# Seven products for eight on a second group of 512 columns of the MLP's second projection, with six PSUM banks holding sums

## The chip, the cores and the metric

The kernel runs on one core of one Trainium2 chip. The metric is the device time of one execution in microseconds. A core has a matrix engine (TensorE, PE in the profile; its weight loads are PEld), a vector engine (VectorE, DVE), a scalar engine (ScalarE, ACT), GpSimd (POOL) and SyncE (SP), which here only starts the loads of the weights. Each engine works off its own list of instructions in a fixed order and waits for the others by semaphores. TensorE writes its sums to PSUM, which has eight banks of 128 x 512 float32 values; VectorE and ScalarE read them from there.

## The reference

Two layers on x of 256 rows and 2048 columns, all in float32. What matters here is the MLP at the end of each layer:

```python
D_MODEL, SEQ, DEPTH, D_FF = 2048, 256, 2, 4 * 2048
for l in range(DEPTH):
    ...                                   # attention and gMLP, output projection, residual
    h2 = rms_norm(x, norm2_g[l])
    x = x + jnp.square(jax.nn.relu(h2 @ w_up[l])) @ w_down[l]
return rms_norm(x, final_g)
```

`w_up` is 2048 x 8192, `w_down` is 8192 x 2048. The result is x of 256 x 2048.

## The kernel before

**Data and precision.** x is kept turned, as `x[128, 16, 256]`. Each float32 operand is split into a high part in the type fp32r and a low part, the remainder. A product of two matrices is made of three products: high by high, high by low, low by high. The weights come in tiles `raw` of 128 x 1024 (512 KB) by SyncE's queue. ScalarE makes the high part (`hi`, L152, or L170 for half a tile), VectorE the low part (`lo`, L162 or L175). There are six buffers for `raw`, seven for `hi`, six for `lo`.

**Steps.** The program is a list `steps`, in the order of TensorE's work. An *ordinary step* (`transposed`) uses one weight tile: 4 blocks of rows by 256 columns, the weights stationary, 24 products of 128 x 128 by 128 x 256 (L380, L382, L384). A bank of PSUM takes the sums of 256 columns: four ordinary steps for `w_up`, two for `w_down`. Then the bank is read: after `w_up` by VectorE at L715, followed by L716, a copy by ScalarE (L611) and a subtraction (L612), together called the *evacuation* here; after `w_down` by the update of x (L471). Ordinary sums rotate through four banks, `acc`.

**Eighths.** The hidden width of 8192 is taken in eight parts of 1024, called eighths, e = 0 to 7. The loop over e puts the 16 up steps of eighth e (numbered 0 to 15) ahead of the down steps of eighth e-1, so that the hidden values are ready in time; e = 8 has the last down steps alone.

**Seven products for eight.** For the first 512 columns of `w_down` the kernel does not multiply directly. Over a pair of row blocks it takes the Winograd form of Strassen's rule: two matrices of 2 x 2 blocks are multiplied with seven block products in place of eight. `fast` makes this of *quick steps*, two in each eighth (a *pair*), with one ordinary step between them. A quick step loads two tiles (`Top`, `Bottom`) and makes two more out of them in place (`Sums`, four subtractions by VectorE, L202, L203, L205, L206). It has 42 products, with the hidden values stationary (L408, L410, L411). So it has one half-tile high and low part and three full ones. The sums of the hidden values that the rule needs are made once an eighth (`sums`, L729 to L732, and four calls of `to_half` into `shared`). The seven block sums lie in the four banks `aux`, half a bank each, and are added up in place through all eight eighths. After the last, `combine` (L744 to L751) makes the four blocks of the result with one copy and seven additions, and `turn_back` turns them by eight transposes (L760), in two sets of four, for the update of x.

**The order of the work.** It is written out by the loop at the end. At each step ScalarE's high parts are put down up to six tiles ahead and VectorE's low parts up to five tiles ahead of `done`, the tiles used so far; a quick step counts as four. Then come the step's products, and what follows the step (`after`: an evacuation, an update). Longer follow-ups lie in `queue` with a number of tiles to let pass (`later`, about one of them a step) or in `due` (`soon`, run ahead of the low parts). VectorE works strictly in this order: an evacuation that waits for TensorE holds up the low parts behind it.

```python
            rest = up or down
            at = {1: (10, 11), 8: (0, 1)}.get(e, (6, 7))
            for i, one in enumerate(rest):
                if quick and i in at:
                    steps.append(quick.pop(0))
                steps.append(one)
```

So a pair stands ahead of up steps 6 and 7 (10 and 11 for e = 1).

## Time and profile before

| | |
|---|---|
| time, median of 3 runs (lowest to highest) | 2054.35 us (2054.31 to 2054.35) |
| the profiled execution, its own time | 2054.54 us |
| its span | 2052.8 us |
| mean granted clock of TensorE in it | 0.998 |
| an eighth, from one pair to the next | 86.0 us (479.87 to 565.86) |
| bytes read from HBM | 390.65 MB, 191 GB/s over the span |

The profile shows one execution. Busy times are the time in which an engine had an instruction at work; the chain that ended last follows the work back from the last instruction to what released it. In rows of the timeline stand the start, the duration, the engine, the line of the code, the instruction, what it writes and reads, and in brackets the idle time ahead of it and what ended it. Products of TensorE overlap: each lasts 0.28 us there, and one starts every 0.11 us.

### The profile page before, as it was taken

Reading aid. Unit: us, or ns where it says so; the run is one execution under the profiler, and the core shown is the slowest. Engines: PE = TensorE matmul, PEld = TensorE weight load, DVE = VectorE, ACT = ScalarE, POOL = GpSimd, SP = SyncE. Lnnn points to the kernel's source line nnn. Section 1 sums busy time; section 2 is a strip of 40 time slices with the busy share of each in tenths; the row PEclk is TensorE's granted clock in tenths of the full one; section 3 lists DMA queues with packets and bytes.
Section 4 is the critical chain, followed back from the end, with each engine's and each line's share of the span. In section 5 each row is a group of like instructions: output and inputs, shape, how many; then the busy total and the mean of one; then the engine's idle time right before and its main releaser. Section 6 shows DMA issues by size and latency. Waiting matters only on the chain.

```text
span 2052.8 us, 40389 instructions
## 1 busy us (share of the span) xinstructions
PE 2040.6 (99%) x17066; PEld 2004.3 (98%) x17066; DVE 1464.6 (71%) x1800; ACT 1009.3 (49%) x1265; POOL 68.0 (3%) x90
## 2 busy tenths in 40 slices
PE   9999999999999999999999999999999999999997
PEld 8998999999999999999989989999999999999997
DVE  7666766777687776877866667668777777777776
ACT  7555454454354443544545654544444544445444
POOL 0002300000000000000000032000000000000000
PEclk9999999999999999999999999999999999999999
DMA  8555555565565655556564555555655756556553
GB/s 317 187 165 174 186 188 193 170 224 193 174 214 178 224 187 184 206 180 211 182 237 159 172 184 177 194 196 172 218 192 168 235 190 202 185 175 224 194 179 113
DMA packets 112118, 395.38 MB, mean 193 GB/s; under 512 B 12352, under 2 KB 16448, under 8 KB 111936
## 3 DMA queue, kind: packets, MB, share of 16 engines
q1 hardware_dynamic: 110800, 389.86, 56.8%
q8 instruction: 133, 2.18, 0.4%
q10 hardware_dynamic: 1136, 2.94, 0.4%
q14 instruction: 49, 0.40, 0.1%
HBM read 390.65 MB, written 2.10 MB: 191 GB/s over the span
## 4 chain that ended last, share of the span: by engine, by line
PE 99%; DVE 0%; DMA 0%; ACT 0%; ACTq 0%; issue 0%; DVEq 0%
PE acc L384 27%; PE acc L382 27%; PE acc L380 27%; PE acc L431 3%; PE acc L433 3%; PE acc L432 3%; PE aux L408 3%; PE aux L411 3%; PE aux L410 3%; PE aux L657 0%; PE aux L601 0%; PE aux L559 0%; PE aux L588 0%; DVE x L876 0%; DMA x<-in_xT 0%; PE aux L562 0%
## 5 line engine op out<-in xcount | busy, mean ns | idle before, releaser
L152 ACT ACTIVATE hi<-raw 128x1024 fp32r<-128x1024 f32 (+1 forms) x773 | 784.1, 1047 | 397.3 <-PE acc L384 211.8
L162 DVE TENSOR_TENSOR lo<-raw,hi 128x1024 fp32r<-128x1024 f32 (+1 forms) x773 | 907.8, 1213 | 42.5 <-ACT hi L152 22.9
L380 PE MATMUL acc<-hs,hi 128*128 128x256 f32 x2816 | 781.5, 278 | 0.0
L384 PE MATMUL acc<-hs,hi 128*128 128x256 f32 x2816 | 779.1, 277 | 0.0
L382 PE MATMUL acc<-hs,lo 128*128 128x256 f32 x2816 | 779.1, 277 | 0.0
L380 PE MATMUL acc<-half,hi 128*128 128x256 f32 x2048 | 566.6, 277 | 0.0
L384 PE MATMUL acc<-half,hi 128*128 128x256 f32 x2048 | 566.1, 276 | 0.0
L382 PE MATMUL acc<-half,lo 128*128 128x256 f32 x2048 | 566.1, 276 | 0.0
L380 PEld LDWEIGHTS acc<-hs,hi 128*128 128x128 f32 x2816 | 529.3, 188 | 0.3 <-issue 0.2
L382 PEld LDWEIGHTS acc<-hs,lo 128*128 128x128 f32 x2816 | 528.9, 188 | 0.4 <-issue 0.2
L384 PEld LDWEIGHTS acc<-hs,hi 128*128 128x128 f32 x2816 | 528.8, 188 | 0.0
L380 PEld LDWEIGHTS acc<-half,hi 128*128 128x128 f32 x2048 | 384.6, 188 | 0.0
L382 PEld LDWEIGHTS acc<-half,lo 128*128 128x128 f32 x2048 | 384.6, 188 | 0.0
L384 PEld LDWEIGHTS acc<-half,hi 128*128 128x128 f32 x2048 | 384.5, 188 | 0.0
L611 ACT ACTIVATE half<-ar 128x512 fp32r<-128x512 f32 x72 | 45.6, 633 | 304.3 <-DVE ar L716 289.7
L471 DVE TENSOR_TENSOR x<-x,acc 128x512 f32<-128x512 f32 (+1 forms) x113 | 76.9, 681 | 160.5 <-PE acc L384 160.5
L715 DVE TENSOR_TENSOR ar<-acc,nR 128x512 f32<-128x512 f32 x64 | 44.3, 692 | 171.7 <-PE acc L384 171.7
L431 PE MATMUL acc<-hi,hs 128*128 128x512 f32 x256 | 101.7, 397 | 0.2 <-ACT hs L269 0.2
L433 PE MATMUL acc<-hi,hs 128*128 128x512 f32 x256 | 100.7, 393 | 0.0
L432 PE MATMUL acc<-lo,hs 128*128 128x512 f32 x256 | 100.0, 391 | 0.0
L612 DVE TENSOR_TENSOR half<-ar,half 128x512 fp32r<-128x512 f32 x72 | 49.9, 693 | 50.6 <-ACT half L611 50.6
L269 ACT ACTIVATE hs<-x,cols 128x256 fp32r<-128x256 f32 x64 | 29.0, 501 | 91.2 <-DVE x L471 90.0
(127 smaller groups left out, 1580.3 us busy)
## 6 DMA issues: line engine op xcount, KB each, us to landing
raw<-in_w SPq DMA_DIRECT2D x731, 512.0 KB, 4.5
raw<-in_w SPq DMA_DIRECT2D x10, 256.0 KB, 5.3
x<-in_xT SPq DMA_DIRECT2D x7, 256.0 KB, 5.8
out<-x SPq DMA_DIRECT2D x7, 256.0 KB, 3.1
shared<-in_b_sp ACTq DMA_DIRECT2D x2, 512.0 KB, 8.0
shared<-in_w_sp ACTq DMA_DIRECT2D x2, 512.0 KB, 9.5
con<-in_consts ACTq DMA_DIRECT2D x1, 512.0 KB, 7.5
x<-in_xT ACTq DMA_DIRECT2D x1, 256.0 KB, 4.4
```

Of the source, the lines that this page charges most:

```text
L152: act.activation(self.h[:, j * m:(j + 1) * m], self.raw[:, j * m:(j + 1) * m], AF.Copy)
L162: vec.tensor_tensor(lo[:, r], self.raw[:, r], self.h[:, r].bitcast(F32), op=OP.subtract)
L380: pe.matmul(o, lhsT=hi, rhs=xs[:, 0, :], start=(k0 + k == 0 and (two or cb == 0)), stop=False, skip_group_check=True)
L382: pe.matmul(o, lhsT=wt.lo[:, k, cb * P:(cb + 1) * P], rhs=xs[:, 0, :], start=False, stop=False, skip_group_check=True)
L384: pe.matmul(o, lhsT=hi, rhs=xs[:, 1, :], start=False, stop=last, skip_group_check=True)
L408: pe.matmul(o, lhsT=xh, rhs=hi, start=(first and p == 0 and k == 0 and n % 2 == 0), stop=False, skip_group_check=True)
L410: pe.matmul(o, lhsT=xh, rhs=lo, start=False, stop=False, skip_group_check=True)
L411: pe.matmul(o, lhsT=xl, rhs=hi, start=False, stop=(last and p == 1 and k == 1), skip_group_check=True)
L431: pe.matmul(ps, lhsT=xh, rhs=hi, start=(k0 + k == 0), stop=False)
L432: pe.matmul(ps, lhsT=xh, rhs=lo, start=False, stop=False)
L433: pe.matmul(ps, lhsT=xl, rhs=hi, start=False, stop=(k0 + k == KC - 1))
L471: vec.tensor_tensor(xj, xj, ps[j][:, 0:S] if alone else pair(ps)[:, j, :], op=OP.add)
```

## The change

A second group of 512 columns of `w_down` (columns 512 to 1023) is done by quick steps too, but only for the first seven of the eight eighths of hidden values; the last is done by ordinary down steps. Each of these eighths has 8 down steps instead of 12, and two pairs of quick steps.

The second group's seven block sums need seven half banks. One is the half of the fourth `aux` bank that was free. Four are the banks `acc` 2 and 3, which hold sums from the second eighth's loop (e = 1) to e = 7. The other two lie in a *spare* bank: whichever of `acc` 0 and 1 is not in use by the up steps around the pair. What is in the spare bank is put into the buffer `kept` after each pair: copied by ScalarE at e = 1 (L795), added by VectorE from then on (L797). The spare bank is then free for the next ordinary sums. So in the MLP ordinary sums rotate through two banks (`of=2`) instead of four, except in the last down steps.

The pairs stand ahead of up steps 1 and 2 (first group) and 9 and 10 (second group); for e = 1 ahead of 9 and 10, and 13 and 14. After the last of them, at e = 7, the second group is recombined (`combine`, now L754 to L761) and turned back through the banks `acc` 2 and 3 (L770), and the update of x (L481) adds it before the last eighth comes.

```diff
-FAST = 512
+FAST = (512, 512)
...
-    pacc = ctx.enter_context(tc.tile_pool(name="pacc", bufs=4, space=bass.MemoryType.PSUM))
+    pacc = ctx.enter_context(tc.tile_pool(name="pacc", bufs=1, space=bass.MemoryType.PSUM))
...
+    kept = ar[:, 3584:3584 + 512]
...
-    def acc_bank():
-        return pacc.tile([P, 512], F32, name="acc", tag="acc")
+    bank_at = [0]
+
+    def acc_bank(i=None, of=4):
+
+        if i is None:
+            i = bank_at[0] = (bank_at[0] + 1) % of
+        return pacc.tile([P, 512], F32, name=f"acc{i}", tag=f"acc{i}")
...
-    def transposed(name, l, row0, nk, col0, ncols, moving, after, between=None, apart=False):
+    def transposed(name, l, row0, nk, col0, ncols, moving, after, between=None, apart=False, of=4):
...
-                    accs[c] = [acc_bank(), acc_bank()] if two else acc_bank()
+                    accs[c] = [acc_bank(of=of), acc_bank(of=of)] if two else acc_bank(of=of)
...
-    def fast(name, l, row0, col0, tiles, banks, first, last, done):
-
+    def fast(name, l, row0, col0, tiles, slots, fresh, last, done):
+
+
+
+        o = []
...
-                if first and p == 0:
-                    banks.extend(aux_bank() for _ in range(4))
+                if p == 0:
+                    o.extend(slots())
...
-                    o = banks[n // 2][:, n % 2 * 256:n % 2 * 256 + 256]
...
-                        pe.matmul(o, lhsT=xh, rhs=hi, start=(first and p == 0 and k == 0 and n % 2 == 0), stop=False,
+                        pe.matmul(o[n], lhsT=xh, rhs=hi, start=(p == 0 and k == 0 and n in fresh), stop=False,
...
-            steps.append(((top, bottom, upper, lower), mm, done if p and last else None))
+            steps.append(((top, bottom, upper, lower), mm, (lambda: done(o)) if p and done else None))
...
-        def combine():
-            p1, p2, p3, p5, p7, p6, p4 = (banks[n // 2][:, n % 2 * 256:n % 2 * 256 + 256] for n in range(7))
+        def combine(o, c, banks, final):
+            p1, p2, p3, p5, p7, p6, p4 = o
...
-            later(2, 1.5, lambda: turn_back(0, c11, c21))
-            later(2, 1.5, lambda: turn_back(2, c12, c22))
-
-        def turn_back(c, first, second):
-            ps = aux_bank()
+            later(2, 1.5, lambda: turn_back(c, c11, c21, banks[0], final))
+            later(2, 1.5, lambda: turn_back(c + 2, c12, c22, banks[1], final))
+
+        def turn_back(c, first, second, bank, final):
+            ps = bank()
...
+        def halves(bank):
+            return [bank[:, 0:256], bank[:, 256:512]]
+
+        held = []
+
+        def slots_all():
+            if not held:
+                held.extend(h for _ in range(4) for h in halves(aux_bank()))
+            return held[0:7]
+
+        most, spare = [], [None]
+
+        def slots_most():
+            if not most:
+                most.extend(h for i in (2, 3) for h in halves(acc_bank(i)))
+            spare[0] = acc_bank(1 - bank_at[0])
+            return most + halves(spare[0]) + held[7:8]
+
+        def keep(e):
+
+            def add(o):
+                if e == 1:
+                    act.activation(kept, spare[0], AF.Copy)
+                else:
+                    vec.tensor_tensor(kept, kept, spare[0], op=OP.add)
+                if e == 7:
+                    later(1, 1.5, lambda: combine(o[0:4] + halves(kept) + o[6:7], FAST[0] // P,
+                                                  [lambda i=i: acc_bank(i) for i in (2, 3)], False))
+
+            return lambda o: soon(1, lambda: add(o))
...
-                up = collect(transposed, "w_up", l, 0, KC, e * 1024, 1024, from_hs, after_up(e))
+                up = collect(transposed, "w_up", l, 0, KC, e * 1024, 1024, from_hs, after_up(e), of=2)
             if e:
...
+                w = sum(FAST[:1 + (e < 8)])
+                hidden = [hid[e - 1]]
+                down = collect(transposed, "w_down", l, (e - 1) * 1024, 8, w, D - w, from_tiles(hidden, NH),
+                               lambda c, ps, e=e, w=w: update(n3, (c + w) // P, ps, e == 8, last),
+                               apart=last and e == 8, of=2 if e < 8 else 4)
+                quick = collect(fast, "w_down", l, (e - 1) * 1024, 0, hidden, slots_all, (0, 2, 4, 6) if e == 1 else (),
+                                e == 8, (lambda o: later(1, 1.5, lambda: combine(o, 0, [aux_bank] * 2, True)))
+                                if e == 8 else None)
+                if e < 8:
+                    quick += collect(fast, "w_down", l, (e - 1) * 1024, FAST[0], hidden, slots_most,
+                                     (0, 2, 4) if e == 1 else (4,), e == 7, keep(e))
             rest = up or down
-            at = {1: (10, 11), 8: (0, 1)}.get(e, (6, 7))
+            at = {1: (9, 10, 13, 14), 8: (0, 1)}.get(e, (1, 2, 9, 10))
```

The lines of the changed kernel stand 8 to 47 further down: L162 becomes L170, L175 L183, L202 to L206 L210 to L214, L380 to L384 L388 to L392, L408 to L411 L418 to L421, L471 L481, L612 L622, L715 L725.

What the change does to VectorE's order is shown at two places in the first layer. The first is in the loop over e = 2, from the last instruction of an evacuation to the end of the pair behind it. Before, it is the evacuation after up step 3 and the pair ahead of up steps 6 and 7:

```order
L612 TENSOR_TENSOR half<-ar,half 128x2x256
L202 TENSOR_TENSOR raw<-raw 128x2x256
L203 TENSOR_TENSOR raw<-raw 128x2x256
L162 TENSOR_TENSOR lo<-raw,hi 128x1024 x3
L175 TENSOR_TENSOR lo<-raw,hi 128x512
L205 TENSOR_TENSOR raw<-raw 128x2x256
L206 TENSOR_TENSOR raw<-raw 128x2x256
L162 TENSOR_TENSOR lo<-raw,hi 128x1024
L202 TENSOR_TENSOR raw<-raw 128x2x256
L203 TENSOR_TENSOR raw<-raw 128x2x256
L162 TENSOR_TENSOR lo<-raw,hi 128x1024 x7
```

Now it is the evacuation after up step 7 and the second group's pair ahead of up steps 9 and 10 (`acc_5688` is the spare bank):

```order
L622 TENSOR_TENSOR half<-ar,half 128x2x256
L170 TENSOR_TENSOR lo<-raw,hi 128x1024 x2
L183 TENSOR_TENSOR lo<-raw,hi 128x512
L213 TENSOR_TENSOR raw<-raw 128x2x256
L214 TENSOR_TENSOR raw<-raw 128x2x256
L170 TENSOR_TENSOR lo<-raw,hi 128x1024
L210 TENSOR_TENSOR raw<-raw 128x2x256
L211 TENSOR_TENSOR raw<-raw 128x2x256
L170 TENSOR_TENSOR lo<-raw,hi 128x1024 x3
L797 TENSOR_TENSOR ar<-ar,acc_5688 128x512
L170 TENSOR_TENSOR lo<-raw,hi 128x1024 x5
```

Two subtractions and one low part that stood behind the evacuation now stand ahead of it. Behind the pair's last low parts and the next step's, VectorE goes on to L797, which reads what the pair's last products wrote; before, it went on to the low parts of the next steps.

The second place is in the loop over e = 7, from the sum into `kept` on. Before, there is only the round of low parts and evacuations:

```order
L715 TENSOR_TENSOR ar<-acc,nR 128x512
L716 SCALAR_TENSOR_TENSOR ar<-ar 128x512
L612 TENSOR_TENSOR half<-ar,half 128x2x256
L162 TENSOR_TENSOR lo<-raw,hi 128x1024 x4
L715 TENSOR_TENSOR ar<-acc,nR 128x512
```

Now the sum, the evacuation after up step 11 and the recombination of the second group:

```order
L797 TENSOR_TENSOR ar<-ar,acc_10823 128x512
L170 TENSOR_TENSOR lo<-raw,hi 128x1024 x5
L725 TENSOR_TENSOR ar<-acc_10792,nR 128x512
L726 SCALAR_TENSOR_TENSOR ar<-ar 128x512
L622 TENSOR_TENSOR half<-ar,half 128x2x256
L755 TENSOR_TENSOR ar<-ar 128x256
L756 TENSOR_TENSOR ar<-ar,acc_4784 128x256
L757 TENSOR_TENSOR ar<-ar 128x256
L758 TENSOR_TENSOR ar<-ar,acc_4785 128x256
L759 TENSOR_TENSOR ar<-ar,acc_4785 128x256
L760 TENSOR_TENSOR ar<-ar,aux 128x256
L761 TENSOR_TENSOR ar<-ar,acc_4785 128x256
```

TensorE has the first set of transposes of this group after up step 13, the second after up step 14.

More of the change, by code (lines that the diff above doesn't have):

```diff
@@ L407, in mm @@
                         hi, lo = b.hi[:, k, cols], b.lo[:, k, cols]
-                        pe.matmul(o, lhsT=xh, rhs=hi, start=(first and p == 0 and k == 0 and n % 2 == 0), stop=False,
+                        pe.matmul(o[n], lhsT=xh, rhs=hi, start=(p == 0 and k == 0 and n in fresh), stop=False,
                                   skip_group_check=True)
-                        pe.matmul(o, lhsT=xh, rhs=lo, start=False, stop=False, skip_group_check=True)
-                        pe.matmul(o, lhsT=xl, rhs=hi, start=False, stop=(last and p == 1 and k == 1),
+                        pe.matmul(o[n], lhsT=xh, rhs=lo, start=False, stop=False, skip_group_check=True)
+                        pe.matmul(o[n], lhsT=xl, rhs=hi, start=False, stop=(last and p == 1 and k == 1),
                                   skip_group_check=True)
-            steps.append(((top, bottom, upper, lower), mm, done if p and last else None))
+            steps.append(((top, bottom, upper, lower), mm, (lambda: done(o)) if p and done else None))
     def natural(name, l, col0, ncols, after):
@@ L760, in turn_back @@
                     pe.transpose(ps[:, o:o + P], src[:, j * P:(j + 1) * P], ident)
-            later(0, 1.5, lambda: update(n3, c, ps, True, last))
+            later(0, 1.5, lambda: update(n3, c, ps, final, last))
+        def halves(bank):
[6 more added lines that the diff above has]
+        most, spare = [], [None]
@@ L763, in layer @@
         base = len(steps)
-        banks = []
         for e in range(9):
-            up, down, quick = [], [], []
+            up, down, quick, more = [], [], [], []
             if e < 8:
-                up = collect(transposed, "w_up", l, 0, KC, e * 1024, 1024, from_hs, after_up(e))
+                up = collect(transposed, "w_up", l, 0, KC, e * 1024, 1024, from_hs, after_up(e), of=2)
             if e:
-                down = collect(transposed, "w_down", l, (e - 1) * 1024, 8, FAST, D - FAST, from_tiles([hid[e - 1]], NH),
-                               lambda c, ps, e=e: update(n3, (c + FAST) // P, ps, e == 8, last), apart=last and e == 8)
-                quick = collect(fast, "w_down", l, (e - 1) * 1024, 0, [hid[e - 1]], banks, e == 1, e == 8,
-                                lambda: later(1, 1.5, combine))
+                w = sum(FAST[:1 + (e < 8)])
[9 more added lines that the diff above has]
+                                     (0, 2, 4) if e == 1 else (4,), e == 7, keep(e))
```

## The prediction

> **What bounds the kernel now.** I read the page first: the span, the busy times and the chain that ended last. Then TensorE's own waits, and last the timeline of TensorE and VectorE around the places that the change touches.
>
> ```profile
> span 2052.8 us, 40389 instructions
> ...
> PE 2040.6 (99%) x17066; PEld 2004.3 (98%) x17066; DVE 1464.6 (71%) x1800; ACT 1009.3 (49%) x1265; POOL 68.0 (3%) x90
> ...
> PE 99%; DVE 0%; DMA 0%; ACT 0%; ACTq 0%; issue 0%; DVEq 0%
> ```
>
> TensorE is busy for 99% of the span and it is the whole chain. TensorE's waits, from the trace:
>
> ```profile
> PE aux L305 <- DVE nr L331: 1.2, 1, 1.2
> PE aux L837 <- DVE warm L833: 1.1, 1, 1.1
> PE acc L431 <- ACT hs L269: 0.2, 1, 0.2
> ```
>
> In 2052.8 us it waits three times, for 2.5 us in all, and never inside the MLP. So a product taken away is a product's time gained, as long as no new wait appears. Busy time says nothing of the rate, since matmuls overlap; starts do. Two rows of TensorE's timeline, 116 products apart in an ordinary stretch:
>
> ```profile
> 439.75 0.28 PE L380 MATMUL acc<-half,hi 128*128 128x256 f32 x1
> ...
> 452.90 0.28 PE L384 MATMUL acc<-half,hi 128*128 128x256 f32 x1
> ```
>
> 13.15 us / 116 = 0.1134 us a product, so an ordinary step (24 products) takes 2.72 us and a bank of two steps 5.44 us.
>
> **What it removes and adds on TensorE.** In each of seven eighths, in two layers (14 times), four ordinary steps of `w_down` (96 products) go and two quick steps (2 x 42 = 84) come: 168 products fewer in all. At 0.1134 us that would be 19.05 us. But a pair of quick steps does not run at that rate. The first starts of the four steps of one pair, before:
>
> ```profile
> 479.87 0.28 PE L408 MATMUL aux<-hi,half 128*128 128x256 f32 x1
> ...
> 484.63 0.28 PE L380 MATMUL acc<-hs,hi 128*128 128x256 f32 x1
> ...
> 487.46 0.28 PE L408 MATMUL aux<-hi,half 128*128 128x256 f32 x1
> ...
> 492.41 0.28 PE L380 MATMUL acc<-hs,hi 128*128 128x256 f32 x1
> ```
>
> The first quick step takes 4.76 us (0.1133 a product). The ordinary step behind it takes 2.83 us and the second quick step 4.95 us, both 0.1179 a product, with no wait recorded. The other 15 pairs start and end at the same distances within a few hundredths. What causes it the trace does not say, so I bound it: the new pairs pay it all, or none of it. I take all of it, since it sits on every pair there is. A new pair then costs 4.76 + 4.95 + (2.83 - 2.72) = 9.82 us and replaces 4 x 2.72 = 10.88: 1.06 us an eighth, **14.8 us** in all. With none of it, 19.05.
>
> Added on TensorE too: in each layer the second group's four blocks are turned back by two more sets of four transposes. One set before, between products:
>
> ```profile
> 1000.11 0.28 PE L384 MATMUL acc<-half,hi 128*128 128x256 f32 x1
> 1000.23 0.60 PE L760 MATMUL aux<-con,ar 128*128 128x128 f32 x4
> ...
> 1000.91 0.28 PE L384 MATMUL acc<-half,hi 128*128 128x256 f32 x1
> ```
>
> From 1000.11 to 1000.91 there are three products, worth 0.34 us, in 0.80: a set costs 0.46 us, four sets **1.84 us**. The Trainium skill ("TensorE: Matmul & The Clock Gate", Part 4) gives some 275 ns for a 128x128 transpose in a kernel; sixteen would be 4.4 us by it and the forecast 2.6 us later. The trace has 0.115 us each between products, so that figure is a latency here, not a price.
>
> **What it adds on VectorE, and what that holds up.** Groups by line and form, and one window of the MLP:
>
> ```profile
> L162 DVE TENSOR_TENSOR lo<-raw,hi 128x1024 fp32r<-128x1024 f32 x763 | 901.3, 1220 | 38.6 <-ACT hi L152 19.0 <-PE acc L432 9.1 <-PE acc L382 3.4
> L471 DVE TENSOR_TENSOR x<-x,acc 128x512 f32<-128x512 f32 x111 | 76.1, 686 | 157.6 <-PE acc L384 157.6
> L203 DVE TENSOR_TENSOR raw<-raw 128x512 f32<-128x512 f32 x32 | 22.2, 693 | 1.1
> L175 DVE TENSOR_TENSOR lo<-raw,hi 128x512 fp32r<-128x512 f32 x32 | 21.9, 686 | 0.0
> ...
> 522.00:610.00 88.00, 88.00 (x776) 88.00 (x775) 64.81 (x74) 40.73 (x46) 0.00 (x0) 1.00 0.59 198
> ```
>
> A quick step needs one low part of 0.69 us, three of 1.22 and four subtractions of 0.69: 7.1 us, against 4.8 us of TensorE. Per eighth VectorE gains 2 x 7.1 + 0.69 (the sum into `kept`) and loses 4 x 1.22 + 2 x 0.69: +8.7 us. It worked 64.8 of 88 us, that is 63.3 of an eighth's 86.0; now 72.0 of 85: 85%. ScalarE, at 40.7 of 88 us, is far from full, and the weights loaded are the same bytes. On average VectorE still fits, so the question is where it is late.
>
> VectorE around a pair, before (times are starts; the evacuation after up-step 3 opens it):
>
> ```profile
> 474.63 0.69 DVE L715 TENSOR_TENSOR ar<-acc,nR 128x512 f32<-128x512 f32 x1 [4.26 <-PE acc L384]
> ...
> 477.36 0.68 DVE L202 TENSOR_TENSOR raw<-raw 128x512 f32<-128x512 f32 x1
> ...
> 486.90 8.20 DVE L162 TENSOR_TENSOR lo<-raw,hi 128x1024 fp32r<-128x1024 f32 x7
> 495.34 0.69 DVE L715 TENSOR_TENSOR ar<-acc,nR 128x512 f32<-128x512 f32 x1 [0.25 <-PE acc L384]
> ```
>
> From 474.63 on it hardly rests for 20 us, but it had 4.26 us to spare ahead of that. Low parts follow each other at 8.20/7 = 1.17 us. The second of the seven, the pair's last, is done at 489.3; TensorE wants it after 30 of the 42 products of the second quick step, at 487.46 + 3.54 = 491.0. Slack: **1.7 us**. In the changed order (first place shown above) the second group's pair has one ordinary step less between the evacuation and the first quick step (2.72 us less time), and one low part and two subtractions less behind the evacuation (1.17 + 1.40 us less work): slack 1.5 us, no stall. The first group's pair now follows the down steps, which end in a light load, and has more. In the first eighth (e=1) the pairs stand close together (steps 9, 10, 13, 14): 4 x 7.1 us of quick-step work with six low parts (7.3) and one evacuation (2.7) are 38.4 us against 2 x 9.82 + 6 x 2.72 = 36.0 of TensorE. The 2.4 us more are about what the slack and a low part made ahead can bear; I take 0 and keep 0 to 1.5 us a layer.
>
> The sum into `kept` waits for the second quick step's last product, and five low parts and an evacuation are queued behind it. That costs nothing in six eighths: an evacuation starts 0.2 us after the next step's first product (474.63 against 479.87 - 5.44), so the next low part is done at 0.2 + 0.69 + 1.22 = 2.1 us, and it is wanted at 2.7. In the seventh it does, by the transposes. The recombination before:
>
> ```profile
> 997.44 0.42 DVE L745 TENSOR_TENSOR ar<-ar,aux 128x256 f32<-128x256 f32 x1 [0.30 <-ACT ar L744]
> ...
> 999.35 0.41 DVE L750 TENSOR_TENSOR ar<-ar,aux 128x256 f32<-128x256 f32 x1
> ```
>
> Its sixth instruction, which the first set of transposes needs, ends 2.32 us after the first starts. Counted from the end of the last quick step, by the two places shown above: 0.2 to the sum, 0.69 for it, 5 x 1.17 for low parts, 2.73 for the evacuation (474.63 to 477.36), 2.32 for the recombination: 11.8 us. TensorE is at the transposes after four ordinary steps, 10.9 us. It waits 0.9 us in each layer: **1.8 us**, between 0 and 3.
>
> Sum: 14.84 - 1.84 - 1.8 = 11.2 us less. The profiled execution took 2054.54 us (span 2052.8 and 1.74 around it), 0.19 above the median of 2054.35; 2054.54 - 11.2 - 0.19 = **2043.1 us**.
>
> **Rivals.**
> *A. Products alone.* The new pairs do not run slow and VectorE is never late: 2054.35 - 19.05 + 1.84 = 2037.1. For it: the cause of the 0.1179 is unknown. Against it: 16 pairs of 16 have it.
>
> *B. VectorE late at each second pair.* If it loses 2 us more than counted, say through the hand-over between ScalarE's high part and VectorE's low one, the slack of 1.5 us turns into 0.5 us of waiting in the 12 pairs of eighths two to seven: 6 us, 2048.9. For it: 85% busy with a work order fixed in advance. Against it: before, with the same chain, TensorE waited at none.
>
> *C. Two banks are too few (slower).* Ordinary sums now rotate through two banks for four, so a bank must be read within the 5.44 us in which the other is filled. Two updates of the running sum `x`, before:
>
> ```profile
> 438.89 0.68 DVE L471 TENSOR_TENSOR x<-x,acc 128x512 f32<-128x512 f32 x1
> ...
> 447.43 0.69 DVE L471 TENSOR_TENSOR x<-x,acc 128x512 f32<-128x512 f32 x1 [0.31 <-PE acc L384]
> ```
>
> The second is on time; two banks earlier, 438.89 stands 2.3 us after 447.43 - 10.88 = 436.55. The limit is 5.44 - 0.69 = 4.75 us, so 2.4 are left, and the decisive point is a VectorE later than 4.75 us behind a filled bank. Then TensorE waits at bank starts: eight an eighth, 112 in all; 0.1 us at each (11.2) eats the gain, 0.2 us (22.4) gives 2065.5. The Trainium skill ("Perfetto Trace Analysis", Matmul Optimizations) asks that all eight PSUM banks be used to keep matmuls and evacuation apart. All eight are still used, but six of them stand still, so by that rule C is the likely case; the 2.4 us in the trace speak against it.
>
> That the change does not do what it says is ruled out by the order: 392 more products stand at each of the quick step's three lines, 448 fewer at each of the ordinary ones.
>
> **How the numbers follow.** Forecast (2041 to 2045.5) 0.5; A and between (2037 to 2041) 0.2; B (2045.5 to 2050.2) 0.18; B worse, no change that counts 0.06; C 0.06. A measurement of this kernel tells 0.2%, some 4 us, from nothing. The range 2036.5 to 2049.0 takes in A and the middle of B. Faster 0.88, same 0.06, slower 0.06.
>
> **What would show it.** Right: products 17066 - 152 = 16914 in all; TensorE's waits list two of some 0.9 us at the transposes of the second group (L770) and little else; pairs in all eighths at 0.1133, 0.1179, 0.1179; VectorE at some 85% in a window of the MLP. Wrong: waits of TensorE at L418 or L420 for low parts (B), waits at L388 of a bank's first product (C), or quick steps at the ordinary rate (A).

## The result, and the profile after

| | before | after |
|---|---|---|
| median of 4 runs, us | 2054.35 | 2041.95 |
| lowest to highest, us | 2054.31 to 2054.71 | 2041.70 to 2042.30 |
| ratio, 95% interval | | 0.9939 [0.9922, 0.9957] |
| profiled execution, us | 2054.54 | 2042.30 |

The change is 12.4 us faster (0.6%); 11.2 were forecast. From the page of the kernel after, the span, the busy times and the chain that ended last; from the trace, all waits of TensorE and one window of the MLP as long as one eighth:

```profile
span 2040.6 us, 40498 instructions
...
PE 2027.7 (99%) x16914; PEld 1991.4 (98%) x16914; DVE 1584.1 (78%) x1970; ACT 1050.8 (51%) x1325; POOL 68.0 (3%) x90
...
PE 99%; DVE 0%; DMA 0%; ACT 0%; ACTq 0%; issue 0%; DVEq 0%
...
PE aux L313 <- DVE nr L339: 1.2, 1, 1.2
PE aux L884 <- DVE warm L880: 1.1, 1, 1.1
PE acc L441 <- ACT hs L277: 0.7, 1, 0.7
...
500.00:585.00 85.00, 85.00 (x747) 85.00 (x746) 71.02 (x82) 42.68 (x48) 0.00 (x0) 1.00 0.58 199
```

TensorE makes the 16914 products that were counted and is still the whole chain. It waits where it waited before, and at no place of the MLP: not for a low part, not for a bank, and not at the new transposes. (The third wait, 6 us from the start, is 0.5 us longer; the first product of 256 columns starts at 51.82 us in both kernels, so nothing is lost by it.) VectorE is busy for 71.0 of 85 us (72.0 forecast).

The four starts of one new pair, from TensorE's timeline after:

```profile
921.56 0.28 PE L418 MATMUL acc<-hi,half 128*128 128x256 f32 x1
...
926.32 0.28 PE L388 MATMUL acc<-hs,hi 128*128 128x256 f32 x1
...
929.15 0.28 PE L418 MATMUL acc<-hi,half 128*128 128x256 f32 x1
...
934.10 0.28 PE L388 MATMUL acc<-hs,hi 128*128 128x256 f32 x1
```

4.76, 2.83 and 4.95 us, to the hundredth what the pair before the change took. So the new pairs inherited the slow stretch, as the sum had it; all 30 pairs read so.

The end of the first layer's MLP is marked by the same small products in both kernels, after and then before:

```profile
1027.50 0.95 PE L305 MATMUL aux<-ones,nacc 128*128 128x1 f32 x8
```

```profile
1033.89 0.94 PE L297 MATMUL aux<-ones,nacc 128*128 128x1 f32 x8
```

That is 6.4 us a layer, 12.8 in two. The sum without its wait at the transposes is 14.84 - 1.84 = 13.0. So the products and the transposes came out as priced, and the wait did not come.

The profiled executions differ by 12.2 us, 0.5 less than this. These 0.5 us lie in the tail. TensorE's last products and their window, after and then before:

```profile
2029.45 1.22 PE L313 MATMUL aux<-con,nr 128*128 128x128 f32 x4 [1.21 <-DVE nr L339]
...
2029.45:2030.67 1.22, 1.22 (x4) 0.93 (x4) 0.00 (x0) 0.00 (x0) 0.00 (x0) 0.50 0.00 0
```

```profile
2042.26 0.71 PE L305 MATMUL aux<-con,nr 128*128 128x128 f32 x4 [1.21 <-DVE nr L331]
...
2042.26:2042.97 0.71, 0.71 (x4) 0.52 (x4) 0.00 (x0) 0.00 (x0) 0.00 (x0) 1.00 0.00 0
```

The same four products take 0.5 us more at a granted clock of 0.50 for 1.00 (the column behind the engines). Both follow a wait of 1.21 us on VectorE, and the change touches none of this code; why the clock fell ahead of these products in one kernel and not in the other is open.

### The profile page after: what moved, and what is told of

Same layout as the page of the kernel before. It is cut to its first block, busy times and chain, and to the rows that moved or that the text cites. A ratio compares the mean times of both kernels' runs of the same rounds, so it can differ in the third digit from the quotient of the medians.

```text
span 2040.6 us, 40498 instructions
## 1 busy us (share of the span) xinstructions
PE 2027.7 (99%) x16914; PEld 1991.4 (98%) x16914; DVE 1584.1 (78%) x1970; ACT 1050.8 (51%) x1325; POOL 68.0 (3%) x90
## 4 chain that ended last, share of the span: by engine, by line
PE 99%; DVE 0%; DMA 0%; ACT 0%; ACTq 0%; issue 0%; DVEq 0%
PE acc L392 25%; PE acc L388 25%; PE acc L390 25%; PE acc L443 3%; PE acc L441 3%; PE aux L418 3%; PE acc L442 3%; PE aux L421 3%; PE aux L420 3%; PE acc L418 2%; PE acc L421 2%; PE acc L420 2%; PE aux L667 0%; PE aux L611 0%; PE aux L569 0%; PE aux L598 0%
## 5 line engine op out<-in xcount | busy, mean ns | idle before, releaser
L160 ACT ACTIVATE hi<-raw 128x1024 fp32r<-128x1024 f32 (+1 forms) x801 | 809.6, 1047 | 411.6 <-DVE raw L214 181.1
L170 DVE TENSOR_TENSOR lo<-raw,hi 128x1024 fp32r<-128x1024 f32 (+1 forms) x801 | 942.1, 1212 | 40.0 <-ACT hi L160 24.3
L388 PE MATMUL acc<-hs,hi 128*128 128x256 f32 x2816 | 781.6, 278 | 0.0
L392 PE MATMUL acc<-hs,hi 128*128 128x256 f32 x2816 | 778.7, 277 | 0.0
L388 PEld LDWEIGHTS acc<-hs,hi 128*128 128x128 f32 x2816 | 529.5, 188 | 0.4 <-issue 0.2
L392 PEld LDWEIGHTS acc<-hs,hi 128*128 128x128 f32 x2816 | 528.6, 188 | 0.0
L388 PE MATMUL acc<-half,hi 128*128 128x256 f32 x1600 | 442.2, 276 | 0.0
L392 PE MATMUL acc<-half,hi 128*128 128x256 f32 x1600 | 441.7, 276 | 0.0
L390 PE MATMUL acc<-half,lo 128*128 128x256 f32 x1600 | 441.7, 276 | 0.0
L388 PEld LDWEIGHTS acc<-half,hi 128*128 128x128 f32 x1600 | 300.4, 188 | 0.0
L390 PEld LDWEIGHTS acc<-half,lo 128*128 128x128 f32 x1600 | 300.4, 188 | 0.0
L392 PEld LDWEIGHTS acc<-half,hi 128*128 128x128 f32 x1600 | 300.4, 188 | 0.0
L725 DVE TENSOR_TENSOR ar<-acc,nR 128x512 f32<-128x512 f32 x64 | 44.1, 689 | 118.0 <-PE acc L392 118.0
L481 DVE TENSOR_TENSOR x<-x,acc 128x512 f32<-128x512 f32 (+1 forms) x89 | 60.2, 676 | 65.8 <-PE acc L392 65.6
L622 DVE TENSOR_TENSOR half<-ar,half 128x512 fp32r<-128x512 f32 x72 | 49.8, 692 | 50.4 <-ACT half L621 50.4
```

What stands on the lines that cost most here:

```text
L160: act.activation(self.h[:, j * m:(j + 1) * m], self.raw[:, j * m:(j + 1) * m], AF.Copy)
L170: vec.tensor_tensor(lo[:, r], self.raw[:, r], self.h[:, r].bitcast(F32), op=OP.subtract)
L388: pe.matmul(o, lhsT=hi, rhs=xs[:, 0, :], start=(k0 + k == 0 and (two or cb == 0)), stop=False, skip_group_check=True)
L390: pe.matmul(o, lhsT=wt.lo[:, k, cb * P:(cb + 1) * P], rhs=xs[:, 0, :], start=False, stop=False, skip_group_check=True)
L392: pe.matmul(o, lhsT=hi, rhs=xs[:, 1, :], start=False, stop=last, skip_group_check=True)
L481: vec.tensor_tensor(xj, xj, ps[j][:, 0:S] if alone else pair(ps)[:, j, :], op=OP.add)
```

## The experiments

Every experiment is an edit of the kernel after, run once, beside one run of the kernel before on the same chip (2054.38 to 2055.45). Differences below are against 2042.30, the profiled execution after. Where each went is read from the starts of TensorE's products in its trace. A distance of 0.1155 to 0.125 us from a product of 256 columns to the next start counts as *slow pitch*. The third column is the sum of what those exceed 0.11334 us, the mean of the distances below 0.1155; the fourth is the rest of the stretch from TensorE's first start to its last; both are against the kernel after.

| run | time, us | slow products | slow pitch, us | waits and the rest, us | measured difference, us |
|---|---|---|---|---|---|
| after | 2042.30 | 2166 | 0 | 0 | 0 |
| e1_adjacent | 2052.21 | 4141 | +8.6 | +1.3 | +9.9 |
| e2_apart | 2047.93 | 3608 | +6.4 | -0.5 | +5.6 |
| e3_turn_early | 2050.74 | 2184 | +0.1 | +8.4 | +8.4 |
| e5_work4 | 2074.86 | 5180 | +13.4 | +19.4 | +32.6 |
| e4_work2 | 2061.68 | 6081 | +17.4 | +2.1 | +19.4 |
| e7_late5 | 2065.57 | 3507 | +6.0 | +17.4 | +23.3 |
| e6_late2 | 2041.96 | 2152 | 0 | -0.1 | -0.3 |
| x2_alternate | 2041.55 | 2168 | 0 | -0.5 | -0.8 |
| x3_ordinary | 2041.39 | 2168 | 0 | -0.7 | -0.9 |
| x4_odd | 2040.95 | 2168 | 0 | -1.3 | -1.4 |
| y1_zero | 2084.43 | 9559 | +32.7 | +9.5 | +42.1 |
| y2_split | 2044.86 | 2138 | -0.2 | +2.9 | +2.6 |

**What the slow stretch is.** It was the one term of the sum without a cause, so the first two runs move the steps of a pair together and apart. In e1_adjacent the two steps of a pair follow each other:

```diff
-            at = {1: (9, 10, 13, 14), 8: (0, 1)}.get(e, (1, 2, 9, 10))
+            at = {1: (10, 10, 14, 14), 8: (1, 1)}.get(e, (1, 1, 10, 10))
             for i, one in enumerate(rest):
-                if quick and i in at:
+                for _ in range(at.count(i) if quick else 0):
                     steps.append(quick.pop(0))
```

> The two quick steps of a pair stand next to each other, with no ordinary step between (first group ahead of up step 1, second ahead of step 10; e = 1: 10 and 14; e = 8: ahead of the second down step). In the changed kernel the ordinary step inside the pair and the second quick step run at 0.1179 us a product, all else at 0.1134. Theory 'between': the slow rate lasts from the end of the first quick step to the end of the second. Then only the 42 products of the second are slow: 24 x 0.0046 us less in each of 30 pairs, 3.3 us less, some 2038.6 us, if VectorE is not late. Theory 'for a time': it lasts some 7.8 us after a quick step; then the second quick step and the ordinary one behind it are slow and the time stays at some 2042. Theory 'second step late': a quick step right behind another finds VectorE late by 1 us or more; waits at L418 or L420 of some 0.5 us in most pairs, 10 us or more.

2052.21 us. In number that is the theory of the late second step, but the trace says otherwise. Its waits in the MLP, and two windows of ordinary steps, the first between the two pairs of an eighth and the second behind both:

```profile
PE acc L420 <- DVE lo L170: 0.5, 1, 0.5
...
476.00:496.00 20.00, 20.00 (x173) 20.00 (x172) 12.53 (x15) 7.46 (x9) 0.00 (x0) 1.00 0.64 240
515.00:535.00 20.00, 20.00 (x179) 20.00 (x179) 15.01 (x18) 9.75 (x12) 0.00 (x0) 1.00 0.70 254
```

One wait of 0.5 us in two layers. But between the pairs TensorE gets 173 products into 20 us, behind them 179, with nothing waiting and a granted clock of 1.00 in both. The first pair of the eighth now runs at 0.1134 throughout; the slow pitch starts behind it, holds for nine ordinary steps and the whole second pair, and ends with that. It is so in all six eighths of the first layer from e = 2 on. None of the three theories had this.

In e2_apart four ordinary steps more stand inside the first pair and one more inside the second:

```diff
-            at = {1: (9, 10, 13, 14), 8: (0, 1)}.get(e, (1, 2, 9, 10))
+            at = {1: (9, 10, 13, 14), 8: (0, 1)}.get(e, (1, 6, 9, 11))
```

> In the loops over e = 2 to 7 the first group's quick steps stand ahead of up steps 1 and 6 (five ordinary steps between), the second group's ahead of 9 and 11 (two between). Theory 'between': all ordinary steps inside run at 0.1179: (4 + 1) x 24 x 0.0046 = 0.55 us more an eighth, 12 times, 6.6 us more, some 2048.5 us. Theory 'for a time': each pair has about 66 slow products as before, then 0.1134 again; some 2042. If the rate belongs to the second quick step alone plus one ordinary step, also some 2042, but the slow products then stand at the second step.

2047.93 us, and a window that lies wholly between the steps of the first pair:

```profile
470.50:483.50 13.00, 13.00 (x113) 13.00 (x112) 7.19 (x10) 3.53 (x4) 0.00 (x0) 1.00 0.36 136
```

13 us hold 113 products here; at 0.1134 they would hold some 115 and the two or three that a window's edges add. Both runs fit one rule: the pitch is a state that stays. Where a run of quick steps ends and an ordinary step follows, it flips; a run of two steps flips it once. The first run of an eighth starts the slow pitch, the next one ends it.

Four runs ask what flips it. In x2_alternate the three products of a quick step come in another order, in x3_ordinary those of an ordinary step, in x4_odd a quick step has 41 products, in y2_split its last product is made as two:

```diff
 x2:                     pe.matmul(o[n], lhsT=xh, rhs=hi, ...)
-                        pe.matmul(o[n], lhsT=xh, rhs=lo, ...)
                         pe.matmul(o[n], lhsT=xl, rhs=hi, ...)
+                        pe.matmul(o[n], lhsT=xh, rhs=lo, ...)
 x3:                     pe.matmul(o, lhsT=hi, rhs=xs[:, 0, :], ...)
-                        pe.matmul(o, lhsT=wt.lo[:, k, cb * P:(cb + 1) * P], rhs=xs[:, 0, :], ...)
                         pe.matmul(o, lhsT=hi, rhs=xs[:, 1, :], ...)
+                        pe.matmul(o, lhsT=wt.lo[:, k, cb * P:(cb + 1) * P], rhs=xs[:, 0, :], ...)
 x4:
+                        if p == 0 and n == 6 and k == 1:
+                            continue
                         pe.matmul(o[n], lhsT=xl, rhs=hi, ...)
 y2:
+                        if p == 0 and n == 6 and k == 1:
+                            for j in (0, P):
+                                pe.matmul(o[n][:, j:j + P], lhsT=xl, rhs=hi[:, j:j + P], ...)
+                            continue
                         pe.matmul(o[n], lhsT=xl, rhs=hi, ...)
```

> In the runs so far the pitch of products is 0.1134 or 0.1179 us, and it flips each time that ordinary steps follow a run of quick steps, once for a run, whether it is one step long or two; so of the two quick steps of a pair the first ends in the slow pitch and the second ends it. Here each three products of a quick step come as xh with hi, xl with hi, xh with lo, so that no stationary tile is used twice running, as in an ordinary step (same sums in another order). Theory 'repeated stationary': the flip comes from that repetition, and is gone: every product at 0.1134, about 30 x 0.305 = 9.2 us less than the change, 2033 us. Theory 'border': the flip comes from the change of roles of weights and x, and stays: 2042 us, slow between the steps of each pair.

> The other way round: each three products of an ordinary step come as hi with xh, hi with xl, lo with xh, so that ordinary steps use a stationary tile twice running, as quick steps do (same sums in another order). Theory 'repeated stationary': what counts is the difference between the two kinds of steps, so the flip is gone here as well, about 2033 us, unless the repetition itself has a pitch of its own in the 8700 products of ordinary steps. Theory 'border': flips at the same places, 2042 us.

> The first step of each pair leaves out its last product (the low part of x in the second k of the seventh product), 41 products for 42. Theory 'parity' (the flip counts products or loads: a border after an odd number does another thing than after an even number): the step between the pair, and the second step, run at 0.1134, 30 x (0.305 + 0.113) = 12.5 us less than the change, 2029.5 us. Theory 'border' or 'repeated stationary' without parity: only the 30 products go, 30 x 0.113 = 3.4 us less, 2038.6 us.

> The last product of the first quick step of each pair is made as two of 128 columns for one of 256 (the same sums). Theory 'the exact phase at the border': another length of the last product changes the phase in which the next one starts, and the flip is gone; with two products of at most 0.113 us for one, each pair gains 0.2 to 0.3 us, 2033 to 2036 us. Theory 'border': only the roles of the two tiles count, the flip stays, and each pair costs up to 0.113 us more: 2042 to 2045.4 us.

2041.55, 2041.39, 2040.95 and 2044.86 us. In all four every pair still runs fast, slow, slow, with 2138 to 2168 slow products for 2166. So neither a stationary tile used twice running, nor an odd number of products, nor the length of the last one is the cause; "border" is what is left standing. What else changes at a border besides the roles of weights and x (the buffers that are read, the banks that are written), no run separates. (x3_ordinary reaches all 13248 products of ordinary steps. x4_odd saves its 3.4 us in the MLP and loses 2.1 in the first 45 us, where TensorE makes 185 products for 194; the edit does not reach there.) x2 and x3 are single runs 0.8 and 0.9 us below the change; between the first and the last product of 256 columns they take the same time to 0.02 us, so nothing is claimed on the difference.

y1_zero puts a small product of another kind behind each first quick step:

```diff
+                if p == 0:
+                    pe.matmul(o[6][0:2, 0:2], lhsT=ident[:, 0:2], rhs=ident[:, 2:4], start=False, stop=False,
+                              skip_group_check=True)
```

> In the runs so far the slow pitch (0.1179 us) did not outlast a set of transposes: where the steps ahead of the set were slow, it was back at 0.1134 after at most six products. Here one small fp32 product of another kind is added as the last of the first quick step of each pair: 2 columns of the identity with 2 others, whose sum is zero, so the result stays as it is. Theory 'border': the flip needs a product of x as stationary tile straight ahead of one of weights as stationary tile; with another kind between them the pitch stays at 0.1134 and each pair gains 0.305 us less the cost of the small product (between nothing and the 0.11 of a 128x128 transpose): 30 x 0.2 to 0.3, 2033 to 2036 us. Theory 'the end of a quick step flips, whatever follows': the pair stays slow, 2042 to 2045.6 us.

2084.43 us, a clear miss, outside what either theory gave. The first pair of the MLP and the start of the next one, from TensorE's timeline, and the same window as above:

```profile
406.89 0.39 PE L388 MATMUL acc<-hs,hi 128*128 128x256 f32 x1
...
409.74 0.28 PE L418 MATMUL aux<-hi,half 128*128 128x256 f32 x1
...
414.51 0.28 PE L388 MATMUL acc<-hs,hi 128*128 128x256 f32 x1
...
422.99 0.28 PE L418 MATMUL acc<-hi,half 128*128 128x256 f32 x1
...
515.00:535.00 20.00, 20.00 (x172) 20.00 (x171) 14.54 (x17) 8.25 (x9) 0.00 (x0) 1.00 0.69 238
```

In the first pair the theory "border" holds: behind the small product the second quick step takes 4.77 us, 0.1136 a product. But its own end, with no small product, now flips the pitch to slow (414.51 to 422.99 for 72 products, 0.1178), and from there up to the transposes at e = 7 nothing flips it back: not the small products, and not the ends of the second steps, which do so in every undisturbed pair of the other runs. Each small product also costs some 0.3 us. So a state with two values and a flip describes the undisturbed pairs of the other runs, but not this run; what the engine holds stays open. (The expectation's premise was not right either: in e7_late5 the slow pitch lasted behind the set of transposes at 957.38 for 23 of the next 24 products and ended at the set after them.)

**Does VectorE bound the second pair next (rival B)?** e5_work4 and e4_work2 add four and two additions (0.72 us each) on VectorE ahead of the last three low parts of the second group's second quick step, in the first six eighths:

```diff
+            for _ in range(self.extra):                       # 4 in e5, 2 in e4
+                vec.tensor_tensor(blocks[:, 0:2, :], t.left(), t.right(), op=OP.add)
```

> Four additions of 128 x 512 (0.72 us each, 2.9 us) that nothing uses are put on VectorE in the second quick step of the second group, in the loops over e = 1 to 6, ahead of the low parts of that step's last two tiles. In the changed kernel's trace the low part for the fourth of the seven products is ready 1.4 us ahead of its use (0.5 us for e = 1). Theory 'VectorE is the next bound': TensorE waits 1.5 us in each of ten pairs and 2.4 us in the two of e = 1, some 20 us more, 2062 us. Rival 'VectorE's 16% of idle time takes it up': within 2 us of 2042.

> Two additions of 128x512 on VectorE (0.69 to 0.73 us each, into a block that is free) for the four of e5_work4, at the same place: ahead of the last low part of the second quick step of the second group, e = 1 to 6 of both layers. In the change that low part is done 1.4 us before TensorE asks for it (0.5 at e = 1). Theory B with its decisive point at 1.4 us: 1.4 us more uses the slack up, and a wait of at most 0.1 us is left from e = 2, 0.9 at e = 1: 2 to 3 us in all, 2042 to 2046 us. Rival, that the slack read from the trace is not there (the low part is needed earlier than the product that names it): some 1.4 us in each of 12 eighths, 2059 us.

2074.86 and 2061.68 us. The waits in the MLP, of e5 and then of e4:

```profile
PE acc L425 <- DVE lo L170: 12.8, 14, 1.0
```

```profile
PE acc L425 <- DVE lo L170: 1.4, 2, 0.7
```

With 2.9 us added, TensorE is held for a low part in each of the 12 eighths (19.4 us in the table's fourth column, for the forecast 20); with 1.4 us only in the first eighth of each layer, 0.7 us. By the waits alone, e4 would be at 2043.7. It is at 2061.7. The second quick step of one of its pairs, the start of the ordinary stretch two eighths later, and two windows between them, one in each eighth:

```profile
505.54 0.28 PE L423 MATMUL acc<-hi,half 128*128 128x256 f32 x1
...
510.60 0.28 PE L391 MATMUL acc<-hs,hi 128*128 128x256 f32 x1
...
684.87 0.28 PE L391 MATMUL acc<-hs,hi 128*128 128x256 f32 x1
...
515.00:535.00 20.00, 20.00 (x173) 20.00 (x172) 14.48 (x18) 9.39 (x11) 0.00 (x0) 1.00 0.70 256
...
600.00:620.00 20.00, 20.00 (x172) 20.00 (x171) 14.55 (x17) 9.19 (x10) 0.00 (x0) 1.00 0.73 256
```

The starts of the same two ordinary stretches in the kernel after the change:

```profile
509.37 0.28 PE L388 MATMUL acc<-hs,hi 128*128 128x256 f32 x1
...
679.26 0.28 PE L388 MATMUL acc<-hs,hi 128*128 128x256 f32 x1
```

The second step takes 5.06 us for 4.95: a stall of 0.11, too short for the list of waits. The ordinary steps behind it then make 173 products in 20 us, where after the change the same stretch makes 179 (as in the row 515 to 535 of e1_adjacent above). The step stays slow behind the stall, and its end, which ends the slow pitch in the kernel after, does not end it here: the next 360 products run slow. Since each later pair flips the pitch twice, the pattern stays turned over: for two eighths the stretches between pairs are slow (172 products from 600 to 620, 179 after the change) and the ordinary step inside a pair is fast. From 510.60 to 684.87 it takes 174.27 us for 169.89, 4.4 us more behind a stall of 0.11, with no wait listed in it. The table says the same of the whole kernel: 17.4 of its 19.4 us are slow pitch, and only 2.1 are the 2 to 3 that were forecast. The decisive point of B was read rightly (1.4 us), its price was not.

**When are two rotating banks too few (rival C)?** After the change the late update of the running sum stands as late as before, 2.3 us (two rows of VectorE's timeline; the second is on time, and two banks of 5.44 us ahead of it is 616.29):

```profile
618.62 0.68 DVE L481 TENSOR_TENSOR x<-x,acc 128x512 f32<-128x512 f32 x1
...
627.17 0.69 DVE L481 TENSOR_TENSOR x<-x,acc 128x512 f32<-128x512 f32 x1 [0.85 <-PE acc L392]
```

e7_late5 and e6_late2 push it back by five and two additions behind the four that make the sums of x:

```diff
             vec.tensor_tensor(a12, a12, a11, op=OP.subtract)
+            for _ in range(5 if hid[1][0] is not None and hid[7][0] is None else 0):      # 2 in e6
+                vec.tensor_tensor(blocks[:, 0:2, :], inner[:, 0:2, :], inner[:, 2:4, :], op=OP.add)
```

> Five more additions on VectorE (128x512, 0.72 us each, into a block that is free) behind the four that make the sums of x, e = 1 to 6 of both layers, so that the update queued behind them, which empties one of the two rotating banks, is 3.6 us later. In the change it is read 2.2 us ahead of the point where its bank is needed. Theory C (two banks, decisive point at 2.2 us): a wait of 1.4 us before the first product of an ordinary step of the up-projection in each of 12 eighths, 17 us, 2059 us. Theory 'VectorE catches up': the update is ahead of its place in the queue by then and the wait is under 0.5 us, below 2048 us.

> Two additions of 128x512 on VectorE for the five of e7_late5, at the same place, so that the update of x queued behind them, which empties a rotating bank, is 1.4 us later. Theory C with its decisive point at 2.2 us: no wait, 2042 us (e7_late5 with 3.6 us had 1.2 to 1.3 us of wait in each eighth). Rival, that the waits of e7_late5 came from something else than the bank's emptying, in proportion to the work added: about two fifths of its waits, 0.5 us in 12 eighths, 2048 us.

2065.57 and 2041.96 us. TensorE's waits in the MLP in e7 (e6 has none), and one of them with the work around it, TensorE's rows and then VectorE's:

```profile
PE acc L388 <- ACT hi L160: 12.7, 10, 1.3
PE acc L388 <- DVE x L481: 1.7, 2, 0.8
...
538.01 0.28 PE L392 MATMUL acc<-half,hi 128*128 128x256 f32 x1
539.56 0.36 PE L388 MATMUL acc<-half,hi 128*128 128x256 f32 x1 [1.27 <-ACT hi L160]
...
537.60 1.22 DVE L170 TENSOR_TENSOR lo<-raw,hi 128x1024 fp32r<-128x1024 f32 x1
538.73 0.68 DVE L481 TENSOR_TENSOR x<-x,acc 128x512 f32<-128x512 f32 x1
...
539.93 1.22 DVE L170 TENSOR_TENSOR lo<-raw,hi 128x1024 fp32r<-128x1024 f32 x1
```

Twelve waits, ten of some 1.3 us; 1.4 in each were forecast. The trace names a high part of ScalarE for ten of them. But the low part of that high part is begun only at 539.93, and TensorE's step runs on from 539.56 without a second wait: it uses a low part that was begun at 537.60 at the latest, and a low part is made from its high part, which was therefore done by then. What else ends just ahead of the product is the update, at 538.73 + 0.68 = 539.41: it is the bank. So the margin lies between 1.4 us (no wait) and 3.6 us (a wait of 1.3), as read: 2.2. The 6.0 us of slow pitch in e7 come on top: at five of the twelve waits the pitch changed, at seven it did not.

**The transposes.** e3_turn_early puts the second group's two sets one ordinary step sooner:

```diff
-            later(2, 1.5, lambda: turn_back(c, c11, c21, banks[0], final))
-            later(2, 1.5, lambda: turn_back(c + 2, c12, c22, banks[1], final))
+            later(2 if final else 1, 1.5, lambda: turn_back(c, c11, c21, banks[0], final))
+            later(2 if final else 1, 1.5, lambda: turn_back(c + 2, c12, c22, banks[1], final))
```

> The second group's transposes come one tile earlier in the order (delay 1 for 2), so TensorE reaches the first set 8.2 us after the last quick step of e = 7, not 10.9. VectorE has the block they need 10.8 us after it in the changed kernel's trace. So TensorE waits some 2.6 us at L770 in each layer: 5.2 us more, some 2047. If VectorE's chain had been hidden by something else than its place in the order (TensorE not waiting because the transposes do not need the recombination's sixth instruction), no wait and some 2042.

2050.74 us. Its waits in the MLP, the place in the first layer in TensorE's timeline, and a window behind it:

```profile
PE acc L770 <- DVE ar L760: 2.4, 2, 1.2
PE acc L770 <- DVE ar L756: 2.1, 2, 1.1
...
944.94 0.55 PE L770 MATMUL acc<-con,ar 128*128 128x128 f32 x3 [1.19 <-DVE ar L760]
945.24 0.36 PE L388 MATMUL acc<-hs,hi 128*128 128x256 f32 x1
...
945.95 0.42 PE L390 MATMUL acc<-hs,lo 128*128 128x256 f32 x1
946.16 0.42 PE L392 MATMUL acc<-hs,hi 128*128 128x256 f32 x1
...
945.60:949.00 3.40, 3.40 (x19) 3.40 (x18) 3.40 (x4) 0.00 (x0) 0.00 (x0) 0.50 0.38 128
```

The waits are there, 2.25 us a layer for the forecast 2.6. But TensorE stands still for most of 2.6 us around them, and afterwards its products start 0.21 us apart at a granted clock of 0.50 for 3.4 us. In both layers together that is the 8.4 us. The Trainium skill ("TensorE: Matmul & The Clock Gate", Part 1) has the clock at half rate after an idle window of some 3.4 us, until a busy window of the same length has passed. The 3.4 us at half rate agree; the idle window does not, since here two waits of 1.1 and 1.2 us with one product between them were enough. So the delay of two was needed, though its margin is small, as the next part shows.

## Why the prediction was right, step by step

- **TensorE bounds, and a product less is a product's time less: right.** 16914 products, 99% busy, no new wait. The 12.8 us of the two MLPs stand against 13.0 of products less transposes.
- **The new pairs run slow: right in size, and now with a rule.** 0.1133, 0.1179, 0.1179 in all 30. The prediction's two ends, all or none, were the right ones to keep apart: rival A (2037.1) needed none. In an undisturbed stream the pitch flips at the end of each run of quick steps; why it does is open, and that the new pairs would do as the old ones was taken over without knowing it.
- **A set of transposes 0.46 us: right.** In the rows below, three products start from 944.88 to 945.56 with a set between them: 0.68 us, less 0.23 for two distances without one, is 0.45. A wait at them would have shown in the list.
- **The wait of 0.9 us a layer at the new transposes: wrong, and the main error of the sum (1.8 us forecast, none seen).** The step that failed is "0.2 to the sum": the sum into `kept` was taken to start 0.2 us after the last quick step's end, as an evacuation does. VectorE's rows after, with TensorE's two behind them:

```profile
933.60 0.69 DVE L797 TENSOR_TENSOR ar<-ar,acc 128x512 f32<-128x512 f32 x1 [1.26 <-PE acc L421]
934.20 5.76 DVE L170 TENSOR_TENSOR lo<-raw,hi 128x1024 fp32r<-128x1024 f32 x5
...
942.59 0.42 DVE L755 TENSOR_TENSOR ar<-ar 128x256 f32<-128x256 f32 x1
...
944.51 0.41 DVE L760 TENSOR_TENSOR ar<-ar,aux 128x256 f32<-128x256 f32 x1
...
944.88 0.28 PE L392 MATMUL acc<-hs,hi 128*128 128x256 f32 x1
945.00 0.60 PE L770 MATMUL acc<-con,ar 128*128 128x128 f32 x4
...
945.56 0.28 PE L390 MATMUL acc<-hs,lo 128*128 128x256 f32 x1
```

The step ends at 934.10 (the pair's rows above), the sum starts at 933.60, 0.5 us *before*. The spare bank holds the fifth and sixth of the seven products, so it is complete six matmuls before the step is, and the sum does not wait for the pair's last products, as said with the change, but for those ahead of them. The sixth instruction of the recombination ends at 944.92; TensorE is there at 945.00. The chain of the prediction, 11.8 us, is 10.8, and TensorE arrives at 10.9. Of the 1.0 us, 0.7 are the earlier start; the other 0.3 are spread over the rows behind it, each a little shorter than the distances that were added up. A margin of 0.1 us decided between 1.8 us and nothing; e3_turn_early, one step sooner, turned it into 2.25 us a layer.

- **VectorE's slack at the second pair, and e = 1 at nothing: right.** 85% busy forecast, 71.0 of 85 us (84%) seen; the slack of 1.5 us is 1.4 by e4_work2. The price of rival B was too low: 0.5 us of wait in 12 eighths was put at 6 us (2043.1 + 6 is 2049.1, not the 2048.9 written there), but e4_work2 paid 19.4 us, 17.4 of them behind its stalls and not in them. Had B come true, the time would probably have lain above the range.
- **Two banks do for the ordinary sums: right.** The 2.4 us of margin are 2.2, and e6_late2 and e7_late5 stand on either side. The rule that the Trainium skill ("Perfetto Trace Analysis", Matmul Optimizations) gives for PSUM banks would have made C the likely case; the runs show no cost as long as the reader stays within the time that the other bank takes to fill.
- **The tail: not foreseen.** The last products at a clock of 0.50 gave 0.5 us back.

1.8 us not paid, less 0.5 in the tail and the 0.2 by which the two MLPs gave less than the sum (12.8 for 13.0), makes the 1.1 us between 2043.1 and the 2041.95 measured. That the margin at the transposes fell on the right side by 0.1 us was luck: the prediction had priced that wait at its length, and in e3_turn_early 2.25 us of it cost 4.2 a layer.

## What to carry to other kernels

When a sum waits "for the end of a step", look for the product inside the step that really releases it: here that was 0.5 us sooner, and it decided a wait. On an engine that is 99% busy, count the distance between starts in each stretch and not only its busy time, since a slow pitch shows in no list of waits. And don't price a new stall at its length: a 0.11 us stall cost 4.4 us by the pitch behind it, and two stalls of 1.1 and 1.2 us were followed by half the clock for 3.4 us.

## What the hardware showed that was not expected

TensorE's products of 128 x 128 by 128 x 256 run in one of two pitches, 0.1134 and 0.1179 us (4% apart), at a granted clock of 1.00 in both. The pitch holds over long stretches, 360 products and more. In an undisturbed stream it flips where ordinary steps (weights stationary) follow quick steps (x stationary), at each of the 30 pairs of the kernel after. It does not flip from ordinary to quick, nor from quick to quick. Stalls disturb this without a rule that these runs show: behind one of 0.11 us in e4_work2 the next border did not end the slow pitch, and of twelve waits of 0.8 to 1.3 us in e7_late5 five changed the pitch. The order of the three products, an odd count and a shorter last product change nothing; a 2-column product at each first border took the first one's flip away, and from that pair's end on the pitch stayed slow up to the transposes at e = 7, since the other borders no longer flipped it back. In the kernel after, 9.9 us of its 2042 are slow pitch (2166 products, 1980 of them in the pairs). A version without it was not found: placing steps so that less lies between two ends, with three quick steps in a row, was not tried.
